# Sliding windows by 16-row bands: 8 KB rows scattered from GpSimd instead of 2 KB pieces from SP and ACT

## The chip, the cores and the metric

The kernel runs on one core of a Trainium2 chip. The metric is the device time of one execution in microseconds; the kernel before takes 212.39 us, the median of three runs (211.13 to 213.55).

## What is computed

The input x has 16 images of 64 channels and 64 x 64 float32 values. An 8 x 8 window moves over each image in steps of 4, so there are 15 x 15 window positions, and each window is copied, all channels together, to a place of its own in the output. No arithmetic is done: it is a copy in which every input value inside the image appears up to four times.

```python
n_h = (h - window_size) // stride + 1      # 15
n_w = (w - window_size) // stride + 1      # 15
result = np.zeros((batch, n_h, n_w, c, window_size, window_size), dtype=np.float32)
for i in range(n_h):
    for j in range(n_w):
        h_start = i * stride
        w_start = j * stride
        result[:, i, j] = x[:, :, h_start:h_start + window_size, w_start:w_start + window_size].copy()
```

The input has 16.78 MB, the output 58.98 MB. For one image and one window position the output is a run of 64 channels x 64 values, 16 KB.

## The kernel before

A partition holds one image's group of 8 channels: 16 images x 8 groups are the 128 partitions (CHI is 8, CLO is 8, lines 30 to 34). The tile L holds the whole input, 128 KB per partition. It is loaded in 8 bands of 8 image rows, each band in 4 DMAs of 2 channels (function load, lines 45 to 47); one such DMA moves 512 KB, in runs of 8 rows x 64 values = 2 KB. The four loads of a band go alternately to the queues of SP and ACT.

The loop over bands n (line 53) makes the windows whose rows are complete once band n is there: one or two window rows i, with all 15 positions j each. While it walks over them it issues the loads of band n + 1, spread evenly among the windows (lines 58 and 59). For each window VectorE copies the 8 x 8 patches of its 8 channels from L into a dense buffer g (line 62, 128 partitions x 512 values), of which there are 36 in turn, and a DMA stores g (line 63), alternately from SP and ACT. A store moves 256 KB; every partition's part is a run of 2 KB in the output, and the 8 partitions of one image lie behind one another there. Each queue runs its issues in program order; a copy waits for its band's loads and for the store that last read its buffer.

Of the kernel before, what the change touches and what calls it, by code (L numbers as in the profile page):

```python
# [1 line left out]

# [4 lines left out]


@with_exitstack  # L10
def kernel(
    ctx: ExitStack,
    tc: tile.TileContext,
    x: bass.AP,
    window_size: int,
    stride: int,
    out: bass.AP,
):
    nc = tc.nc
    P = nc.NUM_PARTITIONS  # L20

    B, C, H, W = x.shape
    Bo, NH, NW, Co, WSo, WSo2 = out.shape
    WS = int(window_size)
    ST = int(stride)
    assert Bo == B and Co == C and WSo == WS and WSo2 == WS

    f32 = mybir.dt.float32

    CHI = P // B  # L30
    CLO = C // CHI
    RB = 8
    NB = H // RB
    assert CHI * B == P and RB == 2 * ST and WS == RB

    lpool = ctx.enter_context(tc.tile_pool(name="lpool", bufs=1))
    gpool = ctx.enter_context(tc.tile_pool(name="gpool", bufs=36))

    L = lpool.tile([P, CLO, H, W], f32)
    x_v = x.rearrange("b (ch cl) (n r) w -> n (b ch) cl (r w)", ch=CHI, n=NB)  # L40
    queues = [nc.sync, nc.scalar]
    NP = 4
    cw = CLO // NP

    def load(n, k):
        cs = slice(k * cw, (k + 1) * cw)
        queues[k % 2].dma_start(out=L[:, cs, n * RB : (n + 1) * RB, :], in_=x_v[n, :, cs, :])  # L47

    for k in range(NP):
        load(0, k)  # L50

    t = 0
    for n in range(NB):
        rows = [i for i in (2 * n - 1, 2 * n) if 0 <= i < NH]
        windows = [(i, j) for i in rows for j in range(NW)]
        every = len(windows) // NP
        for m, (i, j) in enumerate(windows):
            if n + 1 < NB and m % every == 0 and m // every < NP:
                load(n + 1, m // every)
            g = gpool.tile([P, CLO, WS, WS], f32, name="g")  # L60
            src = L[:, :, i * ST : i * ST + WS, j * ST : j * ST + WS]
            nc.vector.tensor_copy(out=g[:, :, :, :], in_=src)  # L62
            queues[t % 2].dma_start(out=out[:, i, j, :, :, :], in_=g[:, :, :, :])  # L63
            t += 1


# [1 line left out]
_INS = ['x', 'window_size', 'stride']  # L68
_OUTS = [((16, 15, 15, 64, 8, 8), 'float32')]

_NUMBERS = {'window_size': 8, 'stride': 4}


# [26 lines left out]
```

## Time and profile before

| | before |
|---|---|
| median of three runs | 212.39 us |
| the profiled execution, its own time | 212.9 us |
| its span, first to last instruction | 211.1 us |
| VectorE | 225 copies, 417 ns each |
| stores | 225 of 256 KB, 113 from SP and 112 from ACT, median 6.1 us from issue to landing |
| loads | 32 of 512 KB, 16 from SP and 16 from ACT, median 6.5 to 7.0 us from issue to landing |

How to read the lines in the prediction. The page gives for each engine its busy time, its share of the span and its number of instructions (DVE is VectorE, POOL is GpSimd, ACT is ScalarE; SPq and ACTq are the queues on which SP and ACT issue DMAs). A line of a DMA queue has the number of packets, the megabytes, and the time that these packets took as a share of the time of all 16 DMA engines. The line that begins with shares by engine sums up the chain of work that ended last. A line of the stretches begins with the stretch in microseconds from the start of the span and its length; then come the busy time and the number of instructions of VectorE and of GpSimd, the clock of the unused TensorE, the mean busy share of the DMA engines, and the GB/s that they moved. When the DMA view is narrowed to a stretch, its shares refer to that stretch. A line of a tile's view gives the smallest, the median and the largest duration of a kind of instruction in nanoseconds, and the start of the first and the last in microseconds.

### The profile page before, as it was taken

The page shows a single profiled execution, that of the slowest core. Times are in us where ns is not written, and L with a number is a line of the kernel's source. Part 1 is how long each engine was busy: PE and PEld are TensorE (multiplying, and loading weights), DVE is VectorE, ACT ScalarE, POOL GpSimd, SP SyncE. Part 2 cuts the span into 40 slices and gives each one's busy share as a digit, 9 for nine tenths or more (in the row PEclk, how much of TensorE's full clock was granted, in tenths as well). Part 3 has the DMA queues.
Part 4 walks back from the last instruction along what each step waited for, and adds up shares of the span by engine and source line. Part 5 has one row for each costly group of instructions (what it writes and reads, how often), then busy time and mean ns, then how long its engine had stood idle before and what let it go on. Part 6 is the DMA issues. An engine that isn't in the chain of part 4 may idle for free.

```text
span 211.1 us, 885 instructions
## 1 busy us (share of the span) xinstructions
DVE 76.2 (36%) x225; POOL 0.2 (0%) x4
## 2 busy tenths in 40 slices
DVE  0299600019700089000692004940029600098000
POOL 0000000000000000000000000000000000000000
DMA  6999999999999999999999999999999999999997
GB/s 213 392 397 405 339 371 373 373 382 339 361 355 348 355 356 399 361 366 330 382 382 366 351 356 382 364 341 338 390 374 347 368 362 385 358 382 364 363 354 243
DMA packets 41112, 75.83 MB, mean 359 GB/s; under 512 B 4113, under 2 KB 4113, under 8 KB 41105
## 3 DMA queue, kind: packets, MB, share of 16 engines
q1 hardware_dynamic: 20624, 38.02, 51.3%
q10 hardware_dynamic: 20480, 37.76, 50.5%
q14 instruction: 8, 0.06, 0.1%
HBM read 16.78 MB, written 58.98 MB: 359 GB/s over the span
## 4 chain that ended last, share of the span: by engine, by line
DMA 73%; DVE 14%; issue 4%; ACTq 0%; DVEq 0%; SPq 0%
DMA out_dram<-g 70%; DVE g L62 14%; DMA L<-in_x_dram 4%; ACTq L47 0%; DVEq L95 0%; ACTq L63 0%; DVEq L62 0%; SPq L63 0%
## 5 line engine op out<-in xcount | busy, mean ns | idle before, releaser
L62 DVE COPY g<-L 128x512 f32<-128x512 f32 x225 | 76.2, 417 | 118.3 <-DMA L<-in_x_dram 101.0
L81 POOL MEMSET const-bfloat16-1.0<- 128x1 bf16 x1 | 0.1, 102 | 0.0
L81 POOL MEMSET const-uint8-127<- 128x1 uint8 x1 | 0.1, 101 | 0.0
L81 POOL MEMSET const-float32-0.0<- 128x1 f32 x1 | 0.1, 99 | 0.2 <-issue 0.2
L81 POOL MEMSET const-float32-1.0<- 128x1 f32 x1 | 0.1, 98 | 0.0
## 6 DMA issues: line engine op xcount, KB each, us to landing
out_dram<-g SPq DMA_DIRECT2D x113, 256.0 KB, 6.1
out_dram<-g ACTq DMA_DIRECT2D x112, 256.0 KB, 6.1
L<-in_x_dram SPq DMA_DIRECT2D x16, 512.0 KB, 7.0
L<-in_x_dram ACTq DMA_DIRECT2D x16, 512.0 KB, 6.5
```

The costliest lines, as they stand in the source:

```text
L62: nc.vector.tensor_copy(out=g[:, :, :, :], in_=src)
L81: nc = _bacc.Bacc("TRN2", target_bir_lowering=False, num_devices=1)
```

## The change

A partition now holds one image, one half of the channels (32, CL) and one band of 16 image rows (HQ is 4 bands): 16 images x 2 halves x 4 bands. Partition number = 8 x image + 4 x half + band. The input is loaded by 16 DMAs of 1 MB, four channel chunks of 8 channels in the order 2, 0, 1, 3, and four bands each; one DMA fills every fourth partition, in runs of 16 rows x 64 values = 4 KB. They alternate between SP and ACT.

A store now takes one window column j and one slot s of 0 to 3, and serves in one go the window rows 4q + s of all four bands q: 60 (j, s) pairs in place of 225 windows. Every partition writes 32 channels x 64 values = 8 KB. For the slots 0 to 2 all 8 window rows lie in the partition's own band and ScalarE copies them. The slot 3 reaches 4 rows into the next band, which is in the next partition: VectorE copies the first 4 rows and fetches the other 4 with a shuffle across partitions. In the last band slot 3 has no window; its rows get an index out of bounds and are dropped.

Since the rows of one store lie at four different window rows, the store is an indirect DMA from GpSimd: a scatter by a list of 128 row numbers, computed at the start in a dozen instructions of one column; the offset of (j, s) is added as a constant. The first 8 pairs are stored in two halves of 16 channels (a 4 KB row each), with the first halves of all eight ahead of the second halves, which alternate with whole windows. That makes 16 half scatters of 0.5 MB and 50 whole ones of 1 MB. The last two pairs are stored by 4 + 3 plain DMAs from SP, one for each band. There are nine buffers of 1 MB, each also usable as two halves. The stores are declared independent of one another.

```diff
@@ -26,42 +26,129 @@
     assert Bo == B and Co == C and WSo == WS and WSo2 == WS
 
     f32 = mybir.dt.float32
-    CHI = P // B
-    CLO = C // CHI
-    RB = 8
-    NB = H // RB
-    assert CHI * B == P and RB == 2 * ST and WS == RB
+    i32 = mybir.dt.int32
+    ALU = mybir.AluOpType
+    HQ = 4
+    CH = P // (B * HQ)
+    CL = C // CH
+    RB = H // HQ
+    NSLOT = RB // ST
+    NWIN = NH * NW
+    CFREE = CL * WS * WS
+    assert HQ == 4 and CH == 2 and WS == 2 * ST
 
     lpool = ctx.enter_context(tc.tile_pool(name="lpool", bufs=1))
-    gpool = ctx.enter_context(tc.tile_pool(name="gpool", bufs=36))
+    ipool = ctx.enter_context(tc.tile_pool(name="ipool", bufs=1))
+    gpool = ctx.enter_context(tc.tile_pool(name="gpool", bufs=1))
 
-    L = lpool.tile([P, CLO, H, W], f32)
-    x_v = x.rearrange("b (ch cl) (n r) w -> n (b ch) cl (r w)", ch=CHI, n=NB)
-    queues = [nc.sync, nc.scalar]
-    NP = 4
-    cw = CLO // NP
 
-    def load(n, k):
-        cs = slice(k * cw, (k + 1) * cw)
-        queues[k % 2].dma_start(out=L[:, cs, n * RB : (n + 1) * RB, :], in_=x_v[n, :, cs, :])
+    L = lpool.tile([P, CL, RB, W], f32)
+    x_v = x.rearrange("b (ch cl) (hq r) w -> hq (b ch) cl (r w)", ch=CH, hq=HQ)
+    NCH = 4
+    cw = CL // NCH
 
-    for k in range(NP):
-        load(0, k)
+    for k in (2, 0, 1, 3):
+        for q in range(HQ):
+            (nc.sync, nc.scalar)[q % 2].dma_start(
+                out=L[q::HQ, k * cw : (k + 1) * cw, :, :],
+                in_=x_v[q, :, k * cw : (k + 1) * cw, :],
+            )
 
-    t = 0
-    for n in range(NB):
-        rows = [i for i in (2 * n - 1, 2 * n) if 0 <= i < NH]
-        windows = [(i, j) for i in rows for j in range(NW)]
-        every = len(windows) // NP
-        for m, (i, j) in enumerate(windows):
-            if n + 1 < NB and m % every == 0 and m // every < NP:
-                load(n + 1, m // every)
-            g = gpool.tile([P, CLO, WS, WS], f32, name="g")
-            src = L[:, :, i * ST : i * ST + WS, j * ST : j * ST + WS]
-            nc.vector.tensor_copy(out=g[:, :, :, :], in_=src)
-            queues[t % 2].dma_start(out=out[:, i, j, :, :, :], in_=g[:, :, :, :])
-            t += 1
+    def itile(name):
+        return ipool.tile([P, 1], i32, name=name)
+    pi, tb, tq, tc_, idx, idx_last = (itile(n) for n in ("pi", "tb", "tq", "tc", "idx", "idx_last"))
+    nc.gpsimd.iota(pi[:, :], pattern=[[0, 1]], base=0, channel_multiplier=1)
+    nc.vector.tensor_scalar(out=tb[:, :], in0=pi[:, :], scalar1=3, scalar2=None, op0=ALU.logical_shift_right)
+    nc.vector.tensor_scalar(out=tc_[:, :], in0=pi[:, :], scalar1=2, scalar2=1, op0=ALU.logical_shift_right, op1=ALU.bitwise_and)
+    nc.vector.tensor_scalar(out=tq[:, :], in0=pi[:, :], scalar1=HQ - 1, scalar2=None, op0=ALU.bitwise_and)
+    nc.vector.tensor_scalar(out=tb[:, :], in0=tb[:, :], scalar1=float(NWIN * CH), scalar2=None, op0=ALU.mult)
+    nc.vector.tensor_tensor(out=tb[:, :], in0=tb[:, :], in1=tc_[:, :], op=ALU.add)
+    nc.vector.tensor_scalar(out=tc_[:, :], in0=tq[:, :], scalar1=float(NSLOT * NW * CH), scalar2=None, op0=ALU.mult)
+    nc.vector.tensor_tensor(out=idx[:, :], in0=tb[:, :], in1=tc_[:, :], op=ALU.add)
+    nc.vector.tensor_scalar(out=tq[:, :], in0=tq[:, :], scalar1=float(HQ - 1), scalar2=float(2 * B * NWIN * CH), op0=ALU.is_equal, op1=ALU.mult)
+    nc.vector.tensor_tensor(out=idx_last[:, :], in0=idx[:, :], in1=tq[:, :], op=ALU.add)
+    HCL = CL // 2
+    idx_h, idx_hlast = itile("idx_h"), itile("idx_hlast")
+    for d, e in ((idx_h, idx), (idx_hlast, idx_last)):
+        nc.vector.tensor_scalar(out=d[:, :], in0=e[:, :], scalar1=2.0, scalar2=None, op0=ALU.mult)
+    o_v = out.rearrange("b i j (ch cl) r w -> (b i j ch) (cl r w)", ch=CH)
+    o_h = out.rearrange("b i j (ch cl) r w -> (b i j ch) (cl r w)", ch=2 * CH)
+    nxt = [min(p + 1, 31) for p in range(32)]
+    order = [(j, s) for j in range(NW) for s in range(NSLOT)]
+    TAIL, BACK = 2, 3
+    o_q = out.rearrange("b i j (ch cl) r w -> i j b ch (cl r w)", ch=CH)
+    def free(st):
+        tc.declare_no_dep(st.ins, group="stores", reason="each store writes rows of its own")
+        tc.add_to_no_dep_group("stores", st.ins)
+    UNITS = 18
+    G = [gpool.tile([P, 2 * HCL, WS, WS], f32, name=f"G{n}") for n in range(UNITS // 2)]
+    at = 0
+    def window(j, s, half):
+        nonlocal at
+        cols = slice(j * ST, j * ST + WS)
+        last = s == NSLOT - 1
+        if half is None:
+            n, c0 = 2, 0
+            at += at % 2
+        else:
+            n, c0 = 1, half * HCL
+        u = at % UNITS
+        at += n
+        cs = slice(c0, c0 + n * HCL)
+        g = G[u // 2][:, u % 2 * HCL : (u % 2 + n) * HCL, :, :]
+        if not last:
+            nc.scalar.copy(out=g, in_=L[:, cs, s * ST : s * ST + WS, cols])
+        else:
+            nc.vector.tensor_copy(out=g[:, :, 0:ST, :], in_=L[:, cs, s * ST : RB, cols])
+            nc.vector.stream_shuffle(out=g[:, :, ST:WS, :], in_=L[:, cs, 0:ST, cols], mask=nxt)
+        if (j, s) in order[-TAIL:]:
+            g_q = g.rearrange("(m q) c r w -> q m (c r w)", q=HQ)
+            for q in range(HQ - 1 if last else HQ):
+                free(nc.sync.dma_start(out=o_q[q * NSLOT + s, j], in_=g_q[q]))
+            return
+        if half is None:
+            o, ix = o_v, (idx_last if last else idx)
+        else:
+            o, ix = o_h, (idx_hlast if last else idx_h)
+        st = nc.gpsimd.indirect_dma_start(
+            out=o,
+            out_offset=bass.IndirectOffsetOnAxis(ap=ix[:, 0:1], axis=0),
+            in_=g.rearrange("p c r w -> p (c r w)"),
+            in_offset=None,
+            element_offset=(s * NW + j) * CH * CFREE + (half or 0) * HCL * WS * WS,
+            bounds_check=B * NWIN * CH * (1 if half is None else 2) - 1,
+            oob_is_err=False,
+        )
+        free(st)
+    EARLY = 8
+    for j, s in order[:EARLY]:
+        window(j, s, 0)
+    late = list(order[:EARLY])
+    rest = list(order[EARLY:])
+    while late:
+        for w in late[:2]:
+            window(*w, 1)
+        for w in rest[:2]:
+            window(*w, None)
+        late, rest = late[2:], rest[2:]
+    for w in rest[:-TAIL]:
+        window(*w, None)
+    at -= 2 * BACK
+    for w in rest[-TAIL:]:
+        window(*w, None)
 
 
 # ---- launch: one core; inputs and outputs as the reference has them ----
```

## The prediction

> **What bounds the kernel now.** I read the page first: engines, DMA packets, queues, chain.
>
> ```profile
> DVE 76.2 (36%) x225; POOL 0.2 (0%) x4
> DMA packets 41112, 75.83 MB, mean 359 GB/s; under 512 B 4113, under 2 KB 4113, under 8 KB 41105
> q1 hardware_dynamic: 20624, 38.02, 51.3%
> q10 hardware_dynamic: 20480, 37.76, 50.5%
> HBM read 16.78 MB, written 58.98 MB: 359 GB/s over the span
> DMA 73%; DVE 14%; issue 4%; ACTq 0%; DVEq 0%; SPq 0%
> ```
>
> The only engine with work is busy 36% of the span. The two queues' packets together take 51.3% + 50.5% = 101.8% of the sixteen DMA engines' time: over 100% because packets of two queues overlap a little. So the transfers are the bound all through, and not a wait on one of them. Of the packets 41105 - 4113 = 36992 carry data, 75.76 MB / 36992 = 2048 bytes each; 4113 are tiny.
>
> Next the stretches: is 359 GB/s all that these engines move?
>
> ```profile
> 0.00:2.00 2.00, 0.00 (x0) 0.20 (x4) 1.00 0.22 14
> 4.00:6.00 2.00, 0.00 (x0) 0.00 (x0) 1.00 1.06 408
> 10.00:20.00 10.00, 10.00 (x31) 0.00 (x0) 1.00 1.06 400
> 22.00:24.00 2.00, 2.00 (x7) 0.00 (x0) 1.00 1.04 315
> 25.00:205.00 180.00, 60.99 (x180) 0.00 (x0) 1.00 1.04 364
> 210.00:211.10 1.10, 0.00 (x0) 0.00 (x0) 1.00 0.00 0
> ```
>
> The last two columns are the DMA share and GB/s. Loads alone (4 to 6 us) run at 408, loads and stores mixed (10 to 20 us) at 400, the long rest, mostly stores, at 364, at the same share. So there the same 2 KB packet takes longer. The DMA view, narrowed to those two stretches, prices it:
>
> ```profile
> DMA packets 2175, 4.00 MB, mean 400 GB/s; under 512 B 223, under 2 KB 223, under 8 KB 2175
> q1 hardware_dynamic: 1092, 2.01, 52.9%
> q10 hardware_dynamic: 1083, 1.99, 52.6%
> ```
>
> ```profile
> DMA packets 35613, 65.57 MB, mean 364 GB/s; under 512 B 3623, under 2 KB 3623, under 8 KB 35606
> q1 hardware_dynamic: 17852, 32.84, 52.0%
> q10 hardware_dynamic: 17754, 32.68, 51.4%
> ```
>
> 10 to 20 us: 105.5% x 10 us x 16 engines = 168.8 us over 2175 - 223 = 1952 data packets, 86.5 ns each (the tiny ones counted as free, here and below). 25 to 205 us: 103.4% x 180 x 16 = 2978 us over 31983, 93.1 ns. The 6.6 ns between them I call the stall. The instruction queue happens to move one 8 KB packet between 49.4 and 49.9 us:
>
> ```profile
> q14 instruction: 1, 0.01, 3.9%
> ```
>
> 3.9% x 0.5 us x 16 = 312 ns for 8 KB, against 4 x 86.5 = 346 ns in 2 KB packets. It is another kind of transfer, but the only longer packet in the trace.
>
> **The change, part by part.** *Packets.* Both kernels move 75.76 MB. Stores become 7200 rows of 8 KB instead of 28800 of 2 KB, loads 4096 rows of 4 KB instead of 8192 of 2 KB. With a fixed part f and v per 2 KB: v + f = 86.5, 4v + f = 312, so v = 75.2 and f = 11.3 ns; a 4 KB packet is 2v + f = 161.7 ns. Each of 16 engines then has 450 x 312 = 140.4 us of stores and 256 x 161.7 = 41.4 us of loads, 181.8 us together. (960 of the rows go out in two halves: 960 x 11.3 / 16 = 0.7 us, left to the bounds.) Before, 36992 / 16 = 2312 packets took 101.8% x 211.1 = 214.9 us (92.9 ns each).
>
> *Stall.* Nothing tells whether it goes with bytes or with packets. With bytes, the stores keep 1800 x 6.6 = 11.9 us; with packets, 450 x 6.6 = 3.0 us. I take the middle, 7.5. Sum 189.3 us.
>
> *Overlap.* DMA works from about 1.5 us (22% of the first 2 us) to 210, 208.5 us, for 214.9 us of packets: 6.4 us are won by overlap. In proportion to time that is 5.7 us afterwards, in proportion to packets (706 against 2312) 2.0; the stores now come mostly from one queue, so not the full share: 4. Leaves 185.3 us.
>
> *Edges.* 1.5 us ahead of the first byte, 1.1 after the last, as now: 2.6.
>
> *Start and handover.* Now the first stores leave at 9.5 us; afterwards the first half-window needs channel chunks 0 and 1, twelve of the sixteen 1 MB loads: 1.5 + 12.6 MB / 0.40 = 33 us. That costs nothing while the loads keep the engines full: sixteen are queued from the start, and the last four (4.2 MB, 10.5 us) cover the first copy, scatter and transfer. Their price:
>
> ```profile
> L62 DVE COPY g<-L x225: 410/416/428, 9.1 to 194.1; 128x512 f32<-128x512 f32 x113
> L63 SPq DMA_DIRECT2D out_dram<-g x113: 538/651/2443, 9.5 to 206.5; - x113
> L63 ACTq DMA_DIRECT2D out_dram<-g x112: 545/669/2047, 9.9 to 204.8; - x112
> ```
>
> A half copy has 1024 elements, at VectorE's rate 2 x 417 ns = 0.83 us; an issue is 0.65 us. Once that cover is gone, a second stretch begins: the late halves need chunk 3, the last load. The eight early halves (4.2 MB) share the engines with it, so both end near 1.5 + 21 MB / 0.4 = 54 us, and then copy plus issue plus first bytes may show: 0 to 3 us, I take 1.
>
> *Copies.* ScalarE takes 39 whole and 12 half windows, VectorE 17 copies and 17 shuffles of the last slot. ScalarE copies are not in the trace; at VectorE's rate a whole one (2048 elements) is 1.67 us, 45 windows' worth 75 us; even at double that, 150 us, they fit the 155 us from 33 us to the end, behind nine buffers (9.4 MB, as many bytes as the 36 of now). Shuffles: 1024 elements, 0.83 us, at four times that still 17 x 4.2 = 71 us with the copies. Both lie beside transfers: nothing. The dozen one-column index instructions lie in the first 33 us. ScalarE's queue issues eight loads ahead of its copies; these wait for loads anyway.
>
> *Issue.* 225 store issues leave SP and ACT; 66 scatters (50 whole, 16 half) come to GpSimd's queue, seven 256 KB stores to SP at the end. GpSimd issues nothing now, so a scatter's price is unknown. From below 0.65 us, an SP issue: 43 us in all, hidden. From above SP's longest, 2.44 us: 33 + 66 x 2.44 + 4.5 us for the last 1.8 MB = 199 us. It is hidden as long as the scatters fit from 33 us to about 184: 151 / 66 = 2.3 us each. A scatter carries 128 rows where an SP store has 128 as well, so I take the low end: nothing. Queued behind a scatter that waits for its copy are all later scatters; the buffers in flight (up to nine, over 20 us of transfers) cover a late copy.
>
> There is a rule in the Trainium skill that speaks against this. SBUF — State Buffer, § SBUF: two separate sides, says that an fp32 SBUF-to-SBUF copy on VectorE can shut GpSimd out of the port through which it writes DMA descriptors. By it, 17 copies of at most 0.83 us would hold scatters up for 14 us in all, each time for less than the transfers queued; as a sum on the path it would be 204 instead of 190. The trace of before has no DMA of GpSimd's and can't show it.
>
> **Sum:** 185.3 + 2.6 + 1 = 188.9 us of span. The profiled run took 212.9 for a span of 211.1, 1.8 outside it, and stands 0.5 above the median of 212.39: 188.9 + 1.8 - 0.5 = **190 us**. Its own bounds: no stall and full overlap give 181.8 - 5.7 + 2.6 + 1.3 = 180; the full stall, little overlap and 3 us of handover 181.8 + 11.9 - 2.0 + 2.6 + 3 + 1.3 = 199.
>
> **The rivals.** *A: bytes, not packets.* The memory side sets 359 GB/s, and bigger packets only wait longer. For it: the store-heavy 180 us stay at 364 whatever VectorE does. Against: 400 over 10 us with both directions in flight, and the cheaper 8 KB packet. Time: 212. The Trainium skill has this rule: HBM Reference, § Specifications (TRN2), gives a core about 358 GB/s. By that rule 75.76 MB take 211.6 us and nothing is won; the mean of 359 agrees, the 400 and 408 don't.
>
> *B: half the gain.* The rows are cut into 4 KB pieces (stores 900 x 161.7 = 145.5 us, 5.1 more), or the stall goes with bytes and stores lose more at the handover: 199 to 207. Cut into 2 KB pieces, the change doesn't do what it says, and A's time comes out.
>
> *C: GpSimd becomes the bound.* Every scatter has 128 computed addresses on one queue. From c = (211 - 33 - 4.5) / 66 = 2.6 us each it is slower than before; at 3.0 us: 33 + 198 + 4.5 + 1.3 = 237. For: nothing in the trace bounds it, and SP's worst issue took 2.44 us. Against: that worst one stood in a full queue; the median is a quarter of it. The Trainium skill, DMA: Bandwidth & Descriptors, § Anatomy of one DMA — SWDGE (gpsimd) path, gives such a DMA about 2.0 us fixed plus bytes over 436 GB/s. One at a time, by that, a whole scatter is 4.4 us and the kernel about 309; but by the same fit the 225 stores of now would take 585 us one at a time, and the span is 211: transfers overlap.
>
> *D: slower loads.* Each load now covers 32 partitions, four apart, where now it is 128. At the slowest stretch's 315 GB/s the 16.8 MB take 11 us more, 201; below 16.78 MB / 64 us = 262 GB/s they would eat the whole gain.
>
> **How the numbers follow.** Forecast 66% (180 to 199), A 5%, B 16%, C 8%, D 5%. The predicted time is the forecast's, 190. From 181 to 207 I leave out A, C, half of D and a little below: about 2 in 10. Runs of before spread by 1%, so that is what counts as a difference. Faster: forecast, B, half of D and a little of A, 86%. Within 1%: most of A, 4%. Slower: C and the worse half of D, 10%.
>
> **What would show it.** Data packets of 8 KB and 4 KB, some 11,300 in place of 36,992; about 315 to 335 ns a store packet; DMA above 400 GB/s from the start to near the end, with no slice under 350 around 40 to 55 us; GpSimd's issues far below 2.3 us each. A: 8 KB packets of 370 ns. B: packets of 4 KB. C: DMA share well below 0.9 from 55 us on, with scatters back to back. D: under 350 GB/s in the first 30 us. A long stretch of idle DMA with GpSimd idle too would show that I missed a wait on a buffer.

## The result, and the profile after

The changed kernel takes 193.48 us (median of four runs, 193.06 to 193.68) against 212.52 for the kernel before (now also four runs, 211.13 to 213.55): a ratio of 0.9105 with a 95% interval of 0.9051 to 0.916. The forecast was 190, with a range of 181 to 207. The profiled execution took 193.68 us for a span of 191.9.

The page of the changed kernel, the lines that answer to those shown of before:

```profile
DVE 30.3 (16%) x62; ACT 86.2 (45%) x52; POOL 64.4 (34%) x71
DMA packets 14196, 75.80 MB, mean 395 GB/s; under 512 B 1936, under 2 KB 1936, under 8 KB 7952
q0 software_dynamic: 9504, 57.15, 73.1%
q1 hardware_dynamic: 2512, 10.22, 13.8%
q10 hardware_dynamic: 2176, 8.39, 11.1%
HBM read 16.78 MB, written 62.65 MB: 414 GB/s over the span
```

The transfers still bound it. The packets took 73.1% + 13.8% + 11.1% = 98.0% of 191.9 us, 188.1 us on each engine, where they took 214.9 before. Data packets fell from 36992 to 14196 - 1936 = 12260; queue 0 is GpSimd's and carries the scatters.

The stretches of the changed kernel; the columns are as before, with ScalarE's busy time put in between VectorE's and GpSimd's:

```profile
5.00:35.00 30.00, 0.00 (x0) 0.00 (x0) 0.00 (x0) 1.00 1.03 412
40.00:68.00 28.00, 5.93 (x12) 24.11 (x19) 20.62 (x22) 1.00 1.02 420
85.00:165.00 80.00, 15.19 (x24) 47.31 (x25) 31.78 (x33) 1.00 1.01 410
1.50:178.00 176.50, 27.92 (x55) 84.34 (x51) 64.10 (x66) 1.00 1.01 410
178.00:191.90 13.90, 1.89 (x3) 1.90 (x1) 0.00 (x0) 1.00 0.69 248
```

Loads alone, the handover, and scatters alone all run at 410 to 420 GB/s, where the kernel before had 364 in its long stretch. Only the last 14 us are worse than before: the engines are busy 69% of them. The prediction put a share over 100% down to two queues; between 85 and 165 us GpSimd's queue alone shows 101.1% (below).

The packet prices, from the DMA view narrowed to the loads (5 to 35 us), and then to the scatters (85 to 165 us):

```profile
DMA packets 3190, 12.35 MB, mean 412 GB/s; under 512 B 176, under 2 KB 176, under 8 KB 3190
q1 hardware_dynamic: 1594, 6.20, 51.4%
q10 hardware_dynamic: 1596, 6.14, 51.2%
```

```profile
DMA packets 4799, 32.83 MB, mean 410 GB/s; under 512 B 792, under 2 KB 792, under 8 KB 792
q0 software_dynamic: 4797, 32.81, 101.1%
```

A 4 KB load packet: 102.6% x 30 x 16 / (3190 - 176) = 163.4 ns (predicted 161.7). An 8 KB scatter packet: 101.1% x 80 x 16 / (4797 - 792) = 323 ns (predicted 312 plus a share of stall, 329).

The groups of instructions and the waits of the changed kernel, for GpSimd and the copies:

```profile
L112 ACT COPY G<-L 128x2048 f32<-128x2048 f32 x39 | 73.8, 1897 | 56.9 <-DMA out_dram<-G,idx_last 25.0 <-DMA out_dram<-G,idx 17.1 <-DVE G L115 13.3
L125 POOL DMA_INDIRECT out_dram<-G,idx x38 | 36.8, 969 | 49.5 <-DMA out_dram<-G,idx 45.6 <-issue 2.8 <-ACT G L112 1.1
L115 DVE STREAM_SHUFFLE G<-L 128x1024 f32<-128x1024 f32 x13 | 16.6, 1278 | 0.0
```

A scatter takes GpSimd 0.97 us, 1.27 us from one start to the next when nothing holds it up, far from the 2.3 us at which it would have been felt; its idle time is mostly spent waiting for earlier scatters, so transfers are always queued. Copies and shuffles take longer than forecast (1.90 and 1.28 us, for 1.67 and 0.83), but within the margins that the prediction left, and are hidden as it says.

### The profile page after: what moved, and what is told of

It reads as the page before. It is cut to its first block, busy times and chain, and to the rows that moved or that the text cites. A ratio compares the mean times of both kernels' runs of the same rounds, so it can differ in the third digit from the quotient of the medians.

```text
span 191.9 us, 458 instructions
## 1 busy us (share of the span) xinstructions
DVE 30.3 (16%) x62; ACT 86.2 (45%) x52; POOL 64.4 (34%) x71
## 2 busy tenths in 40 slices
DMA packets 14196, 75.80 MB, mean 395 GB/s; under 512 B 1936, under 2 KB 1936, under 8 KB 7952
## 3 DMA queue, kind: packets, MB, share of 16 engines
q0 software_dynamic: 9504, 57.15, 73.1%
q1 hardware_dynamic: 2512, 10.22, 13.8%
q10 hardware_dynamic: 2176, 8.39, 11.1%
HBM read 16.78 MB, written 62.65 MB: 414 GB/s over the span
## 4 chain that ended last, share of the span: by engine, by line
DMA 66%; issue 25%; POOL 3%; DVE 1%; POOLq 0%; DVEq 0%; PEldq 0%
DMA out_dram<-G,idx 56%; DMA out_dram<-G,idx_h 9%; POOL out_dram L125 3%; DVE G L115 1%; DVE G L114 0%; POOLq L125 0%; POOL pi L62 0%; DVEq L114 0%; PEldq L182 0%
## 5 line engine op out<-in xcount | busy, mean ns | idle before, releaser
L112 ACT COPY G<-L 128x2048 f32<-128x2048 f32 (+1 forms) x51 | 85.0, 1696 | 59.2 <-DMA out_dram<-G,idx_last 25.0
L125 POOL DMA_INDIRECT out_dram<-G,idx x38 | 36.8, 969 | 49.5 <-DMA out_dram<-G,idx 45.6
L114 DVE COPY G<-L 128x1024 f32<-128x1024 f32 (+1 forms) x17 | 11.0, 646 | 152.8 <-DMA out_dram<-G,idx 88.4
L115 DVE STREAM_SHUFFLE G<-L 128x1024 f32<-128x1024 f32 (+1 forms) x17 | 19.5, 1146 | 0.0
L112 ACT ACT_TABLE_LOAD x1 | 1.3, 1283 | 36.3 <-DMA L<-in_x_dram 36.3
L125 POOL DMA_INDIRECT out_dram<-G,idx_hlast x4 | 4.0, 1001 | 37.7 <-DVE G L115 36.8
L125 POOL DMA_INDIRECT out_dram<-G,idx_last x12 | 11.6, 963 | 11.7 <-DVE G L115 7.8
L125 POOL DMA_INDIRECT out_dram<-G,idx_h x12 | 11.7, 975 | 3.7 <-issue 2.4
```

The lines of the kernel that those rows point to most:

```text
L112: nc.scalar.copy(out=g, in_=L[:, cs, s * ST : s * ST + WS, cols])
L114: nc.vector.tensor_copy(out=g[:, :, 0:ST, :], in_=L[:, cs, s * ST : RB, cols])
L115: nc.vector.stream_shuffle(out=g[:, :, ST:WS, :], in_=L[:, cs, 0:ST, cols], mask=nxt)
L125: st = nc.gpsimd.indirect_dma_start(out=o, out_offset=bass.IndirectOffsetOnAxis(ap=ix[:, 0:1], axis=0), in_=g.rearrange("p c r w -> p (c r ...
```

## The experiments

Four questions were open: what makes the end slow, whether GpSimd's part is really without cost, whether the gain comes from the size of the packets, and what the stall of the kernel before was. The first four runs change the store side of the new kernel. In their edits TAIL is the number of windows at the end that SP stores by plain DMAs. BACK says which buffers the copies of these windows take: with 3, those of the third-last scatter and of the one after it; with 0, those that come free first.

**The last copies earlier.**

```diff
-    TAIL, BACK = 2, 3
+    TAIL, BACK = 2, 0
```

> BACK is 0 instead of 3: the copies of the last two windows go to the buffers that come free first, not to those of the last scatters. Theory (the last copies wait for one of the last scatters, so the DMA engines fall from 410 to about 265 GB/s from 179 us on, some 3.5 us lost): 189 to 191 us, with the plain stores issued before 178 us. Rival (the sixteen engines end the scatters at different times and the end is set by the slowest): 193 to 194 as now.

Measured: 197.62 us, a ratio of 0.9311 (0.9249 to 0.9373) to the kernel before, as are all ratios here: 4 us slower than the changed kernel. Both theories fail. The plain stores did start early, at 168 us, but while they ran beside the last scatters the rate was only 340 GB/s, and the end came later. This run's stretches, and what SP waits for in the end:

```profile
170.00:175.00 5.00, 1.18 (x1) 0.00 (x0) 0.00 (x0) 1.00 1.03 369
175.00:178.00 3.00, 0.00 (x0) 0.00 (x0) 0.00 (x0) 1.00 1.00 339
190.00:192.00 2.00, 0.00 (x0) 0.00 (x0) 0.00 (x0) 1.00 0.31 131
192.00:196.00 4.00, 0.00 (x0) 0.00 (x0) 0.00 (x0) 1.00 0.00 2
```

```profile
SPq L182 <- PEq L182: 3.1, 2, 2.6
```

A full DMA share at 340 GB/s means slow packets, not missing ones. And when scatters are the last transfers, the closing steps of the program last longer: SP's wait in them is 3.1 us here against 0.7 in the changed kernel, where plain stores end it:

```profile
SPq L182 <- PEq L182: 0.7, 2, 0.5
```

So 2.4 us of the 4 are accounted for. (The other runs go the same way, with other sizes: 2.2 us in the run with two queues, which also ends on a scatter; 1.2 in the one with one plain window.)

**No plain stores at all.**

```diff
-    TAIL, BACK = 2, 3
+    TAIL, BACK = 0, 0
...
-        if (j, s) in order[-TAIL:]:
+        if (j, s) in order[len(order) - TAIL :]:
...
-    for w in rest[:-TAIL]:
+    for w in rest[: len(rest) - TAIL]:
...
-    for w in rest[-TAIL:]:
+    for w in rest[len(rest) - TAIL :]:
```

> TAIL is 0: all sixty windows go by scatters from GpSimd, none by SP. Theory (the loss at the end is the wait for a buffer and the small plain stores): 189 to 191 us, the rate at 410 GB/s nearly to the end. Rival (scatters end ragged, and the plain stores at the end repair that): 193 to 196 us.

Measured: 194.45 us (194.33 to 194.62), 1 us slower than the changed kernel: the rival. Its stretches and its closing wait:

```profile
180.00:184.00 4.00, 0.00 (x0) 0.00 (x0) 0.00 (x0) 1.00 1.00 414
184.00:188.00 4.00, 0.00 (x0) 0.00 (x0) 0.00 (x0) 1.00 0.51 215
188.00:192.00 4.00, 0.00 (x0) 0.00 (x0) 0.00 (x0) 1.00 0.05 18
```

```profile
SPq L182 <- PEq L182: 3.1, 2, 2.6
```

With no wait for a buffer in sight, the scatters still end ragged: four microseconds at half the share and half the rate, as if half of the engines were through. The bytes are done some 1.5 us sooner than in the changed kernel (by 189 us, there by 190.3), but the closing steps take 2.4 us more.

**Two queues at once.**

```diff
-    TAIL, BACK = 2, 3
+    TAIL, BACK = 2, 0
...
-        if (j, s) in order[-TAIL:]:
+        if (j, s) in order[-TAIL:] or (half is None and s in (0, 2)):
```

> BACK is 0, and after the start the windows of slots 0 and 2 are stored by four plain DMAs each from SP, only those of slots 1 and 3 by scatters: two queues work beside each other all the time. Theory (packets of two queues overlap: 424 GB/s between 45 and 65 us with two queues against 410 with GpSimd's alone): 3% of 110 us, about 3 us less than the run with BACK 0, 186 to 188. Rival (the rate goes with the bytes, not with the number of queues): the same as that run, 189 to 191. A third way: SP's issues (0.7 us for 256 KB) or its waits cost: over 194.

Measured: 238.01 us, a ratio of 1.1231 (1.1147 to 1.1316): slower than before the change and far from what the theory said. Its premise was a misreading: the 424 GB/s between 45 and 65 us came from one queue, as all but 3 of the 1954 packets of that stretch are GpSimd's. The third way's "over 194" holds; there are waits, as it says, but the packets themselves are slow. The DMA view from 90 to 200 us:

```profile
q1 hardware_dynamic: 3604, 19.64, 55.6%
q0 software_dynamic: 2194, 14.03, 34.4%
```

SP's plain 8 KB packets take 55.6% x 110 x 16 / (19.64 MB / 8192) = 408 ns, the scatters' beside them 353. Nor is it only a matter of two queues at once: in the changed kernel's last stretch, 183 to 190.5 us, when hardly a scatter is left, SP's packets are no faster:

```profile
q1 hardware_dynamic: 335, 1.84, 76.2%
q0 software_dynamic: 34, 0.21, 7.5%
```

76.2% x 7.5 x 16 / (1.84 MB / 8192) = 407 ns. In this run the copies also had to wait for the slow stores' buffers (GpSimd waited 119.9 us for ScalarE's copies), so the 238 is not all packet time.

**All scatters in halves.** Whole windows are replaced by two calls, for half 0 and half 1.

```diff
-            window(*w, None)
+            window(*w, 0)
+            window(*w, 1)
```

> Every scatter is a half one: 116 scatters of 4 KB rows in place of 66. Theory: 8 KB rows cost little less than two 4 KB rows (322 against 2 x 163 ns), which is 1 to 2 us in all; but GpSimd takes 0.96 us and 0.30 us between two, 116 x 1.27 = 147 us from 37.7 us on, so the last scatter is issued near 185 us and GpSimd sets the end: 194 to 198. Rival (the 0.30 us goes away or GpSimd isn't the bound): 191 to 194. If the packet price were 11 ns plus bytes without a stall: 0.8 us more than now.

Measured: 210.55 us (209.03 to 211.84). That GpSimd becomes the bound is right; how much was mis-sized. The waits on GpSimd, and two stretches:

```profile
POOL out_dram L125 <- issue: 42.9, 103, 1.9
```

```profile
100.00:130.00 30.00, 6.57 (x18) 17.53 (x17) 22.38 (x23) 1.00 0.97 379
130.00:140.00 10.00, 2.19 (x6) 4.39 (x5) 4.82 (x5) 1.00 0.64 256
```

23 half scatters in 30 us are 1.30 us each, just too slow for 0.5 MB, and GpSimd hardly waits for transfers any more. The rest of the loss lies in stretches such as 130 to 140 us, where GpSimd stands idle for up to 1.9 us between two scatters; why, the trace doesn't say.

The same run prices a 4 KB scatter packet, from 60 to 80 us, while the engines are still full:

```profile
q0 software_dynamic: 2393, 8.16, 102.3%
```

102.3% x 20 x 16 / (2393 - 400) = 164.3 ns. Two of them are 329 ns against 323 for one packet of 8 KB, so as scatters rows of 4 KB cost the DMA engines hardly more. It is GpSimd's time for each scatter that asks for the 8 KB.

The next two runs take the slow plain packet by itself. Only the plain stores of the last two windows are cut, into 56 DMAs of four 8 KB rows each, meant to use four engines. They differ in which four images go together.

**Four neighbours.**

```diff
+            g_b = g.rearrange("(m k) c r w -> m k (c r w)", k=32)
             for q in range(HQ - 1 if last else HQ):
-                free(nc.sync.dma_start(out=o_q[q * NSLOT + s, j], in_=g_q[q]))
+                for b0 in range(4):
+                    for ch in range(CH):
+                        free(nc.sync.dma_start(out=o_q[q * NSLOT + s, j, 4 * b0 : 4 * b0 + 4, ch], in_=g_b[b0, 4 * ch + q :: 8]))
```

> Only the plain stores of the last two windows are cut up: each DMA stores one channel half of four neighbouring images (4i to 4i+3), so it uses 4 engines with one 8 KB packet each, read from partitions 8 apart. Theory P (a plain store is slow, 408 ns for 8 KB against 322 in a scatter, because two engines that read partitions 32 apart stand in each other's way): here no two partitions are 32 apart, so 305 to 330 ns. Rival H (plain stores are slow because of the memory they write to or of the SP queue): the same here as in the sister run. The total is longer than 193 (56 small DMAs) and says nothing.

Measured, in its DMA view from 184 to 216 us:

```profile
q1 hardware_dynamic: 415, 1.70, 13.1%
```

**Four spread.**

```diff
-            g_b = g.rearrange("(m k) c r w -> m k (c r w)", k=32)
+            g_b = g.rearrange("(m k) c r w -> k m (c r w)", k=32)
...
-                        free(nc.sync.dma_start(out=o_q[q * NSLOT + s, j, 4 * b0 : 4 * b0 + 4, ch], in_=g_b[b0, 4 * ch + q :: 8]))
+                        free(nc.sync.dma_start(out=o_q[q * NSLOT + s, j, b0::4, ch], in_=g_b[8 * b0 + 4 * ch + q]))
```

> The sister run: the same 56 DMAs of 4 packets of 8 KB on 4 engines, but each stores images i, i+4, i+8, i+12, whose partitions lie 32 apart. Theory P: two pairs read partitions 32 apart at the same moment, packets of 450 to 620 ns. Rival H: the same packet time as with neighbouring images, within 20 ns.

Measured, in the same stretch:

```profile
q1 hardware_dynamic: 447, 1.83, 21.1%
```

Neighbours: 13.1% x 32 x 16 / (1.70 MB / 8192) = 323 ns (tiny packets again counted as free). Spread: 21.1% x 32 x 16 / (1.83 MB / 8192) = 484 ns. With the same queue, the same size and four rows to a DMA in both, a packet takes half as long again when the rows are read from partitions 32 apart. (The totals, 221.47 and 217.2 us for one run each, are set by the 56 issues.) The destinations differ too, four neighbouring images against every fourth, so the pair alone does not tell the partitions read from the memory written to. The Trainium skill, SBUF — State Buffer, § Door 1: The DMA port swizzle, says that partitions p and p + 32 lie behind the same one of 16 DMA ports, and DMA: Bandwidth & Descriptors, § The descriptor swizzle, that in a 128-partition transfer into SBUF each engine writes one port. By the first rule the spread stores should collide; by the second the scatters should not, if what it says of writing holds for their reading too. These packet times agree.

The last runs on the prediction's steps start from the kernel before.

**Packets of 1 KB.**

```diff
-            queues[t % 2].dma_start(out=out[:, i, j, :, :, :], in_=g[:, :, :, :])
+            o_v = out[:, i, j, :, :, :].rearrange("b (ch cl) r w -> b ch (cl r w)", ch=CHI)
+            g_v = g.rearrange("p cl r w -> p (cl r w)")
+            for hf in range(2):
+                cs = slice(hf * 256, (hf + 1) * 256)
+                queues[t % 2].dma_start(out=o_v[:, :, cs], in_=g_v[:, cs])
```

> The kernel before, each store cut into two DMAs of 1 KB packets, nothing else. The prediction's price (11.3 ns for each packet besides its bytes): 28800 more store packets, 1800 for each engine, 20 us more: 230 to 236 us. Rival A (the time goes with the bytes): 212 to 215. If every packet of a store also brings its own stall of 6.6 ns: 12 us more on top, 242 to 248.

Measured: 245.29 us, a ratio of 1.154 (1.1478 to 1.1602), in the third of the ranges, that of a stall for each packet. Its queues:

```profile
q1 hardware_dynamic: 36896, 38.03, 49.5%
q10 hardware_dynamic: 36608, 37.76, 49.3%
```

Packets cost, so bytes alone (rival A) are out. How much each costs is less plain. 32.7 us for 1800 more packets on each engine are 18.2 ns for a packet, and the prediction's 11.3 and 6.6 make 17.9. But the packets' own time rose only from 214.9 us to 98.8% x 242.9 = 240.0, which is 13.9 ns for each further packet; the rest goes with the engines' mean share, which fell from 101.8% to 98.8%. So the run doesn't show that every packet brings a stall of 6.6 ns.

**All loads first.** The band loads are all issued ahead of the first window.

```diff
-    for k in range(NP):
-        load(0, k)
+    for n in range(NB):
+        for k in range(NP):
+            load(n, k)
...
-            if n + 1 < NB and m % every == 0 and m // every < NP:
-                load(n + 1, m // every)
```

> The kernel before with all 32 loads issued ahead of the first window, nothing else: first loads alone, then stores alone, as in the changed kernel. Theory M (the 2 KB stores are slowed by loads that come in between): stores alone then run at 400 GB/s too, 198 to 203 us. Theory P (the plain stores slow one another): stores alone stay at 355 to 370 GB/s, loads alone run at 410, and the total is 205 to 214.

Measured: 215.04 us, a ratio of 1.0139 (1.0068 to 1.021). Its stretches:

```profile
20.00:30.00 10.00, 1.72 (x6) 0.00 (x0) 1.00 1.05 387
60.00:100.00 40.00, 20.77 (x55) 0.00 (x0) 1.00 1.03 362
100.00:200.00 100.00, 43.96 (x115) 0.00 (x0) 1.00 1.03 354
```

Stores with no load among them still run at 354 to 362 GB/s, as theory P has it. Mixing was not the cause of the stall; the new order of loads brought nothing by itself. Two parts of theory P's forecast missed: loads alone ran at 387 GB/s, not 410, and the total lies just above its 205 to 214.

**The stores of before as scatters.** Row numbers are computed from the partition as in the change, 2 KB a row.

```diff
-            queues[t % 2].dma_start(out=out[:, i, j, :, :, :], in_=g[:, :, :, :])
+            st = nc.gpsimd.indirect_dma_start(
+                out=o_v,
+                out_offset=bass.IndirectOffsetOnAxis(ap=idx[:, 0:1], axis=0),
+                in_=g.rearrange("p c r w -> p (c r w)"),
...
+                element_offset=(i * NW + j) * CHI * CLO * WS * WS,
```

> The kernel before with its 225 stores issued by GpSimd as scatters of 128 rows of 2 KB by computed rows, nothing else. GpSimd sets the time, 225 x 1.27 us = 286 us plus 10, some 296, so only the packets count. Theory P (2 KB stores stall by 6.6 ns because engines of a plain store read partitions 32 apart, and a scatter's engines don't): the scatters' 2 KB packets take 84 to 87 ns, as loads do. Rival (2 KB stores to this memory stall by themselves): 91 to 94 ns, as now.

Measured: 308.81 us in one run. Its packets from 30 to 300 us, and two stretches:

```profile
q0 software_dynamic: 17036, 55.84, 54.2%
```

```profile
10.00:60.00 50.00, 24.87 (x66) 36.99 (x35) 1.00 1.04 406
60.00:280.00 220.00, 69.78 (x161) 167.56 (x173) 1.00 0.57 215
```

54.2% x 270 x 16 / (55.84 MB / 2048) = 85.9 ns for 2 KB, which looks like theory P. But 17036 packets, of which 211 scatters x 16 = 3376 are tiny ones, for 55.84 MB are 4 KB each: two neighbouring rows travel as one packet. Such a packet takes 171 ns, more than the 163.4 of a 4 KB load, though after 60 us the engines are only half busy. So the run has no 2 KB store packet to judge theory P by, and leaves it open. It shows the price of scatters that are too small: 173 of them in 220 us are 1.27 us each, and GpSimd sets the time.

**The copies on VectorE.**

```diff
-            nc.scalar.copy(out=g, in_=L[:, cs, s * ST : s * ST + WS, cols])
+            nc.vector.tensor_copy(out=g, in_=L[:, cs, s * ST : s * ST + WS, cols])
```

> The changed kernel with ScalarE's 51 copies moved to VectorE, nothing else: VectorE is then busy for some 90 us with copies. By the rule that such a copy shuts GpSimd out, a scatter that meets one takes up to 1.3 us longer than 0.96: GpSimd's busy time rises from 64 us towards 100, but a scatter stays under the 2.3 us that the transfers of 1 MB allow, so 193 to 196 us. Rival (no such effect): scatters stay at 0.96 to 1.1 us and the time at 193 to 194. Second rival (VectorE's order of work holds scatters up): over 196.

Measured: 193.47 us (193.11 to 194.12), the same as the changed kernel. The scatters in the view of the output, this run's first and the changed kernel's second:

```profile
L125 POOL DMA_INDIRECT out_dram<-G,idx x38: 959/1384/1950, 51.9 to 166.6; - x38
```

```profile
L125 POOL DMA_INDIRECT out_dram<-G,idx x38: 962/962/1049, 50.7 to 166.6; - x38
```

A VectorE copy does hold a scatter up, by 0.4 us in the median and 1.0 at most, as the Trainium skill's rule of the shared port has it (SBUF — State Buffer, § SBUF: two separate sides). GpSimd is busy for 85.1 us in place of 64.4, and the transfers ahead of it hide that fully.

**Two other endings.** In one TAIL is 1, in the other BACK is 4; nothing else.

```diff
-    TAIL, BACK = 2, 3
+    TAIL, BACK = 1, 3
```

> TAIL is 1: only the very last window is stored by plain DMAs from SP (0.79 MB), the one ahead of it by a scatter. Theory (1 MB less goes out in packets of 404 ns at 290 GB/s, and GpSimd's closing 2.4 us still lie beside the plain stores): 1 to 2 us less than now, 191.5 to 192.5. Rival (the ragged end of the scatters only comes later): 193 to 194.5.

```diff
-    TAIL, BACK = 2, 3
+    TAIL, BACK = 2, 4
```

> BACK is 4 instead of 3: the last two windows' copies wait for scatters one earlier, so the plain stores begin some 2.5 us sooner, while the scatters' ragged end (179 to 183 us at half the rate) still runs. Theory (they fill the idle half of the engines): 1 us less, 192 to 193. Rival (plain stores beside scatters slow both, as with BACK 0): 193.5 to 195.

Measured: 193.41 (192.86 to 193.48) and 193.42 us (193.09 to 193.64): no difference from 193.48 that can be told. Both theories fail; the first rival's range holds, the second's begins just above. In the first the rate falls off just as before; its stretches:

```profile
180.00:184.00 4.00, 1.65 (x3) 0.00 (x0) 0.00 (x0) 1.00 0.77 324
184.00:188.00 4.00, 0.25 (x1) 0.00 (x0) 0.00 (x0) 1.00 0.75 252
```

None of the experiments gives a version that beats the changed kernel.

## Why the prediction came out right, and where it was off

**Direction and mechanism** hold: the DMA engines are the bound, a packet has a price of its own beside its bytes (run of 1 KB packets), and neither GpSimd, the copies, the shuffles nor the strided loads cost anything. D is out (loads at 412). A is out: the mean is 395 GB/s, and 410 over 176.5 us. (The section of the Trainium skill that the prediction names for A, HBM Reference, § Specifications (TRN2), itself excepts a core that streams alone, at about 425 GB/s; the 410 here agrees with the exception.) B is out: 14196 - 7952 = 6244 packets have the full 8 KB. C lies well away at whole scatters (1.27 against 2.3 us), though the runs with small scatters show that it is real.

**The sum of the packets** was 189.3 us; the page has 188.1. Within it, the loads were 1% and the scatter rows 2% off.

**Stall.** The choice "with bytes or with packets" left out how the store is issued, and the middle between them came near by luck. By the prediction's prices the scatters keep (323 - 312) x 450 = 5 us of stall, where 3.0, 7.5 and 11.9 stood to choose from. But for the same 8 KB rows a plain band store's packet takes 407 ns. At that price 450 packets would take 183 us, more than the 1800 x 93.1 ns = 168 us of the 2 KB stores of before. Longer rows in such plain stores would thus have lost time: an estimate, as no run did all stores so; the run that did about half was 12% slower than the kernel before, in part through its waits. So the indirect store, which I costed as an issue only, is what lets the longer rows pay here. A plain packet need not be slow: in the stores of four neighbours it took 323 ns too, but those are issues of 32 KB each, far too many.

Of the 26.8 us of packet time that went away, 1546 fewer packets make 17.5 at 11.3 ns, or 21.5 at the 13.9 ns of the run of 1 KB packets. That the other 5 to 9 us are a smaller stall is an inference; no run shows it by itself. That partitions 32 apart cause the slow plain packet is likely from the two runs of four rows, not shown, since their destinations changed too; for the 2 KB stores of before it is a guess. One thing speaks against taking it further: the new kernel's loads are plain DMAs into every fourth partition, some of them 32 apart as well, and at 163.4 ns they lose nothing. Whether writing differs from reading there, or the packets are dealt out to the engines differently, no run shows.

**Handover.** I took 1 us; there is none, 420 GB/s from 40 to 68 us. The first copy started at 36.3 us, not 33, and that cost nothing either, since the last loads cover it.

**Overlap and edges** are where the 3 us between 188.9 and 191.9 lie. Overlap was taken as 4 us; at a share of 1.01 over 176.5 us it is about 1.8. The end was taken "as now", 1.1 us; but from 178 us on the engines are busy for 0.69 x 13.9 = 9.6 us of the 12.3 until the bytes stop, 2.7 us lost, and the closing after the last byte takes 1.6. A sum of packet times cannot see that: it takes all sixteen engines as busy to the end. With the scatters' end at half the engines' share even where no buffer is waited for (the run without plain stores), the likely reading is that the engines come through their scatters at different times; the plain stores behind them are slow besides. My first explanation for this, the late buffers, fell: earlier copies, one plain window, none, and one more step back made it no better. What sets some engines back stays open, since the trace doesn't name an engine for each packet.

## What to carry to other kernels

When DMA is busy all the time, divide the queues' share by the data packets: the time of a packet, stretch by stretch and queue by queue, shows what a longer row or another way to issue can win. Do not take a packet's price from one kind of DMA over to another: measure the same row from each queue. And a scatter from GpSimd needs enough bytes: at 1.3 us from one to the next, 1 MB is hidden (193.5 us) and 0.5 MB is not (210.6).

## What was not expected of the hardware

- A plain store of 8 KB rows from every fourth partition takes 407 ns a packet, the same rows in a scatter 323. In stores of four rows it is 484 when the partitions lie 32 apart (and the images four apart), else 323.
- A kernel that ends on scatters closes later: SP's wait in the closing steps was 2.2 to 3.1 us in three such runs, and 0.7 in the changed kernel, which ends on plain stores.
- The page's line on HBM counts 62.65 MB written. That is 3.67 MB more than the output, just the 14 x 32 rows of 8 KB that are dropped as out of bounds; the packets add up to 75.80 MB with no such rows, so the 414 GB/s of that line is too high.
- A scatter of 2 KB rows that are neighbours in the output moves two rows in one 4 KB packet (171 ns).
